# RWKV-7 branch of a hybrid decoder layer: the keys' norm applied in the channels' layout instead of at the evictions

## The chip, the cores and the metric

The kernel runs on one core of a Trainium2 chip. Its engines work side by side, each through its own list of instructions in order: TensorE (PE) multiplies matrices, VectorE (DVE) and ScalarE (ACT) work on elements, GpSimd (POOL) helps, and SyncE (SP) issues nearly all transfers (DMAs). The metric is the time of one execution in device microseconds (us).

## The reference

One step of one layer: 512 prompt tokens and 8 samples of 8 tokens (576 tokens in all) with 1024 channels. After a norm and one wide input projection, three branches run (RWKV-7, a gated linear recurrence, cross-attention), each with a gate; they are merged, projected and added to the input. The change lies in the RWKV-7 branch, which has 16 heads of 64 channels:

```python
kk = heads(k * k_k)
kk = kk * lax.rsqrt(jnp.sum(kk * kk, axis=-1, keepdims=True) + L2_EPS)   # norm over the 64 channels of a head
k = k * (1.0 + (a - 1.0) * k_a)
def step(s, inp):                       # per token; s is 64 x 64 for each head
    r_t, k_t, v_t, w_t, kk_t, a_t = inp
    sa = jnp.einsum("bhvk,bhk->bhv", s, -kk_t)
    s = s * w_t[:, :, None, :] + sa[..., None] * (kk_t * a_t)[:, :, None, :] + v_t[..., None] * k_t[:, :, None, :]
    return s, jnp.einsum("bhvk,bhk->bhv", s, r_t)
```

So each token and head has one number, the inverse squared norm of its key, that has to reach the products of kk. The kernel keeps kk without its norm on one side and multiplies that number in on the other.

## The kernel before

**Tiles.** The recurrence is done in 9 chunks of 64 tokens: 8 of the prompt, and one (c = 8) that holds the 8 samples. Heads go in pairs (a pair's 128 channels are the 128 partitions, tokens lie along the free axis); two pairs make a group, and four groups follow one another. For each group the program runs these stages, named as in the code:

- `prep_a`, for each pair: the low-rank products (`lora`, L909 and L910), tanh of them on ACT (L911), the running sum of the log decay as a scan on DVE (L914), its exponentials `pe` and `tw` on ACT (L918 to L920), the negated keys `lc` (L921) and their squares `sq` (L923).
- `prep_b`: nine matmuls per pair (`rs`, L932) sum the squares over the channels of a head. A token of the chunk is then a partition and (chunk, head) the free index, 64x18 in all. DVE turns the sums into `rsv`, the reciprocal with its factor (L935, L936). Then DVE builds `ZR` (L940 to L943) and `BK` (L944 to L948): the two sides of the chunk products.
- `prep_c`: `BKn`, the keys decayed to the chunk's end (L969 on ACT, the sample chunk at L970 on DVE), transposed on PE (`bkt`) beside the values (`vt`), in steps of 4, 4 and 1 chunks. ACT evicts `vt` (L977); DVE evicts `bkt` times `rsv` (L981), where the token is the partition again. Then the chunk products `m` (L990, four matmuls of 64x64x128 per chunk, 36 per pair) go to PSUM and DVE evicts them into `M1`, one 128x128 block at a time, times `rsv` of that token and head, times a mask (L996, 18 per pair).
- `invert`: the diagonal 32x32 blocks of `M1` go to DRAM and come back with one block per partition (L1006, L1011), are inverted by 60 small DVE operations (L1016, L1018) and written back (L1025 to L1032). Meanwhile `direct` (`R`, L1065, and `Zt`) and `bonus` run, and `invert2` finishes with `z` and `w` (L1041, L1050). Then the chain over the chunks follows, and at its end `gn_a`, the next group's `prep_a`, and `gn_t` and `gn_b`, which transpose, scale and gate the output (`ot`, `oT`): ACT evicts `oT` (L1240), POOL adds the bonus (L1245), DVE gates it (L1247), SP writes it out as `oad`.

**Filler.** All wide projections (input columns `u`, `za`, `g`, `br` and so on) are units of 48 matmuls at L355 (float32 split into a high and a low part). They do not depend on the recurrence, so `st.go(n)` and `st.until` place them between its stages to keep PE at work. Their weights come as `wraw` and are split by ACT (`whi`, L280) and DVE (`wlo`, L281).

**Order.** Each engine runs its own list in order. The build layer's scheduler sets these lists from the dependencies and its estimates, so the order of an engine's instructions is not that of the code. All PSUM tiles of the recurrence (`rs`, `lora`, `ot`, `vt`, `bkt`, `m`, `R`, `z`) take turns on four banks of one ring: a tile of this ring can only be written when the one four places earlier has been evicted.

Of the kernel before, what the change touches and what calls it, by code (L numbers as in the profile page):

```python
# [9 lines left out]
F32 = mybir.dt.float32  # L10
# [3 lines left out]
ALU = mybir.AluOpType  # L14
# [4 lines left out]
P = 128  # L19
# [5 lines left out]
N = TP + NB * NS  # L25
HN = N // 2
C = 64
NCH = N // C
# [6 lines left out]
L2_EPS = 1e-12  # L35
# [766 lines left out]
def rwkv_phase(K):  # L802
    nc, tc, i, pv, st = K.nc, K.tc, K.i, K.pv, K.st
    G = 2
# [3 lines left out]
    with ExitStack() as es:  # L808
# [9 lines left out]
        pe = [pe2[:, q, :] for q in range(G)]  # L818
        rsv = [rc.tile([P, NCH, 2], F32, name=f"rsv{q}") for q in range(G)]
        onat = rc.tile([P, NCH, P], F32, name="onat")  # L820
# [10 lines left out]
        for q in range(G):  # L831
            nc.gpsimd.memset(pe[q][:, 0:520].rearrange("p (c t) -> p c t", t=65)[:, :, 0:1], 1.0)
            nc.gpsimd.memset(pe[q][:, 520:592].rearrange("p (c t) -> p c t", t=9)[:, :, 0:1], 1.0)
            nc.gpsimd.memset(rsv[q][64 * q:64 * q + 64], 1.0)
            nc.gpsimd.memset(sbd[q], 0.0)
# [5 lines left out]
        x = (K.xh, K.xl)  # L841
# [39 lines left out]
        def chk(t):  # L881
            return t.rearrange("p (c t) -> p c t", t=C)
# [16 lines left out]
        def prep_a(o):  # L899
# [24 lines left out]
            o.pinv, o.zn, o.ta, o.sq = tw, lc, ta, sq  # L924

        def prep_b(o):
            p, q = o.p, o.q
            br = o.br
            zs = 1 - q
            pr_ = K.psb("rs")  # L930
            for c in range(NCH):
                nc.tensor.matmul(pr_[br:br + 64, 2 * c:2 * c + 2], o.sq[:, C * c:C * c + C], K.bones2, start=True, stop=True,  # L932
                                 tile_position=(0, br))
            rvf = rsv[q][br:br + 64].rearrange("p c h -> p (c h)")
            nc.vector.tensor_scalar(rvf, pr_[br:br + 64, 0:18], -2.0, -2.0 * L2_EPS, op0=ALU.mult, op1=ALU.add)  # L935
            nc.vector.reciprocal(rvf, rvf)  # L936
            BK = o.BK = rg.tile([P, NCH, 2, C], F32, tag="BK", name="BK")
# [5 lines left out]
            nc.vector.tensor_mul(ZR[:, 8, q, :].rearrange("p (b s) -> p b s", s=NS), smp(o.r), o.Ps[:, :, 1:])  # L943
            nc.vector.scalar_tensor_tensor(sq, ta, 1.0, zn, op0=ALU.add, op1=ALU.mult)  # L944
            nc.vector.tensor_mul(BK[:, :, zs, :], chk(sq), chk(o.pinv))
            nc.scalar.activation(ta, ta, AF.Identity, scale=K.kah[:, p:p + 1], bias=K.kac[:, p:p + 1])
# [16 lines left out]
        def prep_c(o):  # L963
            q, BK, ZR = o.q, o.BK, o.ZR
            rv = rsv[q]
            UV = o.UV = UV2[0][:, q]
# [6 lines left out]
            for c0, n in ((0, 4), (4, 4), (8, 1)):  # L973
# [5 lines left out]
                for c in range(c0, c0 + n):  # L979
                    K.transpose(pt[:, P * (c - c0):P * (c - c0) + P], BKn[:, c], P)  # L980
                nc.vector.tensor_mul(BKn[:, c0:c0 + n, :].rearrange("p c (h k) -> p (c h) k", h=2),  # L981
                                     pt[:, 0:P * n].rearrange("p (g k) -> p g k", k=C),
                                     rv[:, c0:c0 + n, :].rearrange("p c h -> p (c h)").unsqueeze(2).to_broadcast([P, 2 * n, C]))
            M1 = o.M1 = rg.tile([P, H2, P], F32, tag="M1", name="M1")
            for c0, n in ((0, 4), (4, 4), (8, 1)):
# [8 lines left out]
                for h in range(2):  # L994
                    for c in range(c0, c0 + n):
                        nc.vector.scalar_tensor_tensor(M1[:, 2 * c + h, :], pms[h][:, P * (c - c0):P * (c - c0) + P],  # L996
                                                       rv[:, c, h:h + 1], maskq[q][c == 8],
                                                       op0=ALU.mult, op1=ALU.mult)

# [508 lines left out]
```

## Time and profile before

| what | value |
|---|---|
| time, median of 3 runs | 1182.16 us (1181.98 to 1182.41) |
| the profiled execution | 1184.47 us, with a span of 1182.7 us |
| PE busy | 1145.4 us, 97% of the span |
| DVE busy | 713.2 us, 60% |
| ACT busy | 517.3 us, 44% |
| POOL busy | 184.3 us, 16% |
| first to last `rs` product | 276.8 us to 748.6 us |

The profile shows one execution. Busy time is the time in which an engine had an instruction under way; "idle before" is the time for which an instruction's engine had nothing to do ahead of it, with what released it. The span is from the first to the last instruction, and the 1.8 us beside it are start and end. A row of the trace gives its start in us, its length in us, the engine, the line of the code, and the tile written and the tiles read; "x4" stands for four like it in a row.

### The profile page before, as it was taken

What the parts mean: (1) busy time and instruction counts of PE and PEld (TensorE: products, weight loads), DVE (VectorE), ACT (ScalarE), POOL (GpSimd) and SP (SyncE); (2) the same over time, 40 slices, a digit from 0 to 9 for tenths busy, and PEclk for the clock granted to TensorE, in tenths of its full rate; (3) what the DMA queues carried; (4) which work ended last, traced back from release to release, by engine and by line L of the source; (5) the groups of instructions that cost most, each with busy time, mean ns of one, the idle gap of its engine ahead of it and who ended that gap; (6) DMA issues with size and microseconds to landing.
All of it is one profiled execution on the core that took longest, in us unless ns stands there. A gap on an engine that the chain in (4) does not pass through costs nothing.

```text
span 1182.7 us, 25731 instructions
## 1 busy us (share of the span) xinstructions
PE 1145.4 (97%) x10567; PEld 1068.8 (90%) x10567; DVE 713.2 (60%) x1436; ACT 517.3 (44%) x1004; POOL 184.3 (16%) x311
## 2 busy tenths in 40 slices
PE   6999999999999999999999999999999999979997
PEld 4998877899998898988989989999889999979997
DVE  5345655238764687835788457874455386975633
ACT  5444544337324374243752336532444266442333
POOL 3010001010003210022100130101211012570031
PEclk9999999999999999999999999999999999998999
DMA  4447685522452233532233522345337665348412
GB/s 140 130 145 233 211 254 189 162 81 66 107 140 73 65 93 82 142 89 70 78 92 120 145 73 65 106 125 149 85 90 232 203 195 170 104 115 261 117 45 81
DMA packets 220623, 151.50 MB, mean 128 GB/s; under 512 B 52640, under 2 KB 196106, under 8 KB 220506
## 3 DMA queue, kind: packets, MB, share of 16 engines
q1 hardware_dynamic: 217242, 146.87, 42.1%
q10 hardware_dynamic: 3264, 2.99, 0.9%
q8 instruction: 83, 1.36, 0.5%
q14 instruction: 34, 0.28, 0.1%
HBM read 120.82 MB, written 29.01 MB: 127 GB/s over the span
## 4 chain that ended last, share of the span: by engine, by line
PE 79%; DVE 7%; ACT 5%; issue 3%; DMA 3%; POOL 2%; SPq 0%; DVEq 0%; ACTq 0%; POOLq 0%
PE u L355 13%; PE g L355 12%; PE br L355 9%; PE xb L355 4%; PE zc L355 4%; PE za L355 4%; PE fo L1349 4%; PE q L355 4%; PE zb L355 3%; PE kv L355 2%; PE m L990 1%; PE dS L1137 1%; DVE wlo L281 1%; DMA wraw<-in_w_mem_kv 1%; PE skt L64 1%
## 5 line engine op out<-in xcount | busy, mean ns | idle before, releaser
L280 ACT CAST whi<-wraw 128x1024 fp32r<-128x1024 f32 x129 | 135.4, 1050 | 292.6 <-PE g L355 90.7
L281 DVE TENSOR_TENSOR wlo<-wraw,whi 128x1024 fp32r<-128x1024 f32 x128 | 158.9, 1241 | 127.5 <-ACT whi L280 126.7
L355 PE MATMUL u<-xh,whi 128*128 128x288 f32 x400 | 92.2, 305 | 0.0
L355 PE MATMUL br<-oh,wlo 128*128 128x288 f32 x384 | 84.4, 302 | 4.4 <-DVE wlo L281 4.3
L355 PE MATMUL u<-xl,whi 128*128 128x288 f32 x400 | 88.6, 300 | 0.0
L355 PE MATMUL u<-xh,wlo 128*128 128x288 f32 x400 | 88.6, 299 | 0.0
L355 PE MATMUL br<-oh,whi 128*128 128x288 f32 x384 | 85.4, 305 | 3.0 <-ACT oh L592 2.9
L355 PE MATMUL g<-xh,whi 128*128 128x288 f32 x384 | 86.6, 304 | 0.0
L355 PE MATMUL g<-xh,wlo 128*128 128x288 f32 x384 | 84.7, 300 | 0.0
L355 PE MATMUL g<-xl,whi 128*128 128x288 f32 x384 | 84.4, 301 | 0.0
L355 PE MATMUL br<-ol,whi 128*128 128x288 f32 x384 | 84.2, 301 | 0.0
L355 PEld LDWEIGHTS u<-xh,whi 128*128 128x128 f32 x400 | 65.1, 188 | 5.5 <-issue 4.1
L355 PEld LDWEIGHTS br<-oh,wlo 128*128 128x128 f32 x384 | 63.5, 194 | 5.6 <-DVE wlo L281 5.6
L355 PEld LDWEIGHTS br<-oh,whi 128*128 128x128 f32 x384 | 63.7, 193 | 4.3 <-ACT oh L592 3.4
L355 PEld LDWEIGHTS u<-xl,whi 128*128 128x128 f32 x400 | 64.7, 188 | 2.0 <-issue 1.4
L355 PEld LDWEIGHTS u<-xh,wlo 128*128 128x128 f32 x400 | 64.7, 188 | 0.9 <-issue 0.2
L355 PEld LDWEIGHTS g<-xh,whi 128*128 128x128 f32 x384 | 62.3, 190 | 3.2 <-issue 3.1
L355 PEld LDWEIGHTS g<-xh,wlo 128*128 128x128 f32 x384 | 62.7, 190 | 1.2 <-issue 1.2
L355 PEld LDWEIGHTS br<-ol,whi 128*128 128x128 f32 x384 | 63.4, 193 | 0.1
L355 PEld LDWEIGHTS g<-xl,whi 128*128 128x128 f32 x384 | 62.4, 190 | 1.1 <-issue 1.1
L1016 DVE TENSOR_TENSOR Xt<-X 72x30 f32<-72x30 f32 (+14 forms) x120 | 39.3, 328 | 11.4 <-DMA X<-d 7.8
L1349 PE MATMUL fo<-wol,oh 128*128 128x256 f32 (+1 forms) x160 | 45.0, 282 | 0.0
(386 smaller groups left out, 2894.3 us busy)
## 6 DMA issues: line engine op xcount, KB each, us to landing
wraw<-in_w_in SPq DMA_DIRECT2D x89, 512.0 KB
wraw<-in_w_mem_kv SPq DMA_DIRECT2D x16, 512.0 KB
kn<-in_cache_mem_k SPq DMA_DIRECT2D x16, 512.0 KB
kn<-in_cache_mem_v SPq DMA_DIRECT2D x16, 512.0 KB
gd<-flt SPq DMA_DIRECT2D x24, 288.0 KB
gtt<-gd SPq DMA_DIRECT2D x24, 288.0 KB
wraw<-in_w_br_c SPq DMA_DIRECT2D x8, 512.0 KB
wraw<-in_w_br_a SPq DMA_DIRECT2D x8, 512.0 KB
```

What stands on the lines that cost most here:

```text
L64: self.nc.tensor.transpose(out, in_, self.ident[:rows, :rows])
L280: nc.scalar.copy(hi, raw)
L281: eng.tensor_sub(lo, raw, hi.bitcast(F32))
L355: nc.tensor.matmul(self.ps[:, o:o + m], a[:, k, :], b[:, k, t0:t0 + m], start=(k == 0 and q == 0), stop=(k == KC - 1 and q == 2))
L990: nc.tensor.matmul(pms[h][64 * w:64 * w + 64, P * (c - c0):P * (c - c0) + P], BK[64 * h:64 * h + 64, c, w, :], ZR[64 * h:64 * h + 64, c].r ...
L1016: nc.vector.tensor_mul(tv, X[:, 0:s, s:s + 1].to_broadcast([NQ, s, m]), X[:, s:s + 1, s + 1:].to_broadcast([NQ, s, m]))
L1137: nc.tensor.matmul(pS[hs, C * o.q:C * o.q + C], o.BKn[:, c, hs], o.UV[:, c, hs], start=True, stop=True, tile_position=(0, 64 * h))
L1349: nc.tensor.matmul(pos[t][:r, :W], a[:, k, t * P:t * P + r], b[:, k, :], start=(k == 0 and q == 0), stop=(k == KC - 1 and q == 2))
```

## The change

It does three things.

1. The norm's reciprocal is applied once in the channels' layout. The nine `rs` matmuls, the scaling and the reciprocal move from `prep_b` to the end of `prep_a`. The result (64 tokens x 18) is written to a DRAM tile `d4` transposed (each of its 1152 elements goes to an address of its own; L936 in the changed file), and read back twice (L939), each time one head's row of 576 numbers spread over that head's 64 partitions, into the tile `sq`, whose squares are no longer needed. In `prep_b`, `sq` is multiplied by `pinv` (the tile `tw`), `(ta + 1) * zn` is written to `BK` directly, and `BK` is multiplied by `sq`: three DVE operations of 128x576 where there were two.
2. The eviction of the transposed `BKn` is a plain copy, and ACT does it (L989) instead of DVE.
3. The eviction of `m` into `M1` multiplies by the mask alone, four chunks at a time: 6 operations per pair (four of 128x4x128, two of 128x128; L1001) instead of 18.

`rsv` has its two heads outside the chunks now, and its initial fill with ones is gone.

```diff
--- before.py
+++ after.py
@@ -816,7 +816,7 @@
         ue = [rc.tile([P, UE], F32, name=f"ue{q}") for q in range(2)]
         pe2 = rc.tile([P, G, PE_], F32, name="pe")
         pe = [pe2[:, q, :] for q in range(G)]
-        rsv = [rc.tile([P, NCH, 2], F32, name=f"rsv{q}") for q in range(G)]
+        rsv = [rc.tile([P, 2, NCH], F32, name=f"rsv{q}") for q in range(G)]
         onat = rc.tile([P, NCH, P], F32, name="onat")
         sbd = [rc.tile([P, G, P], F32, name=f"sbd{r}") for r in range(2)]
         sbs = rc.tile([P, NB, P], F32, name="sbs")
@@ -831,7 +831,6 @@
         for q in range(G):
             nc.gpsimd.memset(pe[q][:, 0:520].rearrange("p (c t) -> p c t", t=65)[:, :, 0:1], 1.0)
             nc.gpsimd.memset(pe[q][:, 520:592].rearrange("p (c t) -> p c t", t=9)[:, :, 0:1], 1.0)
-            nc.gpsimd.memset(rsv[q][64 * q:64 * q + 64], 1.0)
             nc.gpsimd.memset(sbd[q], 0.0)
 
         xw2 = [rc.tile([P, N], F32R, name=f"xw{n}") for n in range(2)]
@@ -923,17 +922,26 @@
             nc.scalar.activation(sq, lc, AF.Square)
             o.pinv, o.zn, o.ta, o.sq = tw, lc, ta, sq
 
+            br = o.br
+            pr_ = K.psb("rs")
+            for c in range(NCH):
+                nc.tensor.matmul(pr_[br:br + 64, 2 * c:2 * c + 2], sq[:, C * c:C * c + C], K.bones2, start=True, stop=True,
+                   tile_position=(0, br))
+            rv = rsv[q][br:br + 64]
+            nc.vector.tensor_scalar(rv.rearrange("p h c -> p c h"), pr_[br:br + 64, 0:18].rearrange("p (c h) -> p c h", h=2),
+                                    -2.0, -2.0 * L2_EPS, op0=ALU.mult, op1=ALU.add)
+            rvf = rv.rearrange("p h c -> p (h c)")
+            nc.vector.reciprocal(rvf, rvf)
+            d4 = dr.tile([18, C], F32, tag="d4", name="d4")
+            nc.sync.dma_start(d4.rearrange("x t -> t x"), rvf)
+            d4h = d4.rearrange("(h c) t -> h (c t)", h=2)
+            for h in range(2):
+                nc.sync.dma_start(sq[64 * h:64 * h + 64, :], d4h[h:h + 1, :].to_broadcast([64, N]))
+
         def prep_b(o):
             p, q = o.p, o.q
             br = o.br
             zs = 1 - q
-            pr_ = K.psb("rs")
-            for c in range(NCH):
-                nc.tensor.matmul(pr_[br:br + 64, 2 * c:2 * c + 2], o.sq[:, C * c:C * c + C], K.bones2, start=True, stop=True,
-                                 tile_position=(0, br))
-            rvf = rsv[q][br:br + 64].rearrange("p c h -> p (c h)")
-            nc.vector.tensor_scalar(rvf, pr_[br:br + 64, 0:18], -2.0, -2.0 * L2_EPS, op0=ALU.mult, op1=ALU.add)
-            nc.vector.reciprocal(rvf, rvf)
             BK = o.BK = rg.tile([P, NCH, 2, C], F32, tag="BK", name="BK")
             ZR = o.ZR = rg.tile([P, NCH, 2, C], F32, tag="ZR", name="ZR")
             zn, ta, sq = o.zn, o.ta, o.sq
@@ -941,8 +949,9 @@
             nc.vector.tensor_mul(ZR[:, 8, zs, :].rearrange("p (b s) -> p b s", s=NS), smp(zn), o.Ps[:, :, 0:NS])
             nc.vector.tensor_mul(ZR[:, 0:8, q, :], chk(o.r)[:, 0:8, :], o.Pp[:, :, 1:])
             nc.vector.tensor_mul(ZR[:, 8, q, :].rearrange("p (b s) -> p b s", s=NS), smp(o.r), o.Ps[:, :, 1:])
-            nc.vector.scalar_tensor_tensor(sq, ta, 1.0, zn, op0=ALU.add, op1=ALU.mult)
-            nc.vector.tensor_mul(BK[:, :, zs, :], chk(sq), chk(o.pinv))
+            nc.vector.tensor_mul(sq, sq, o.pinv)
+            nc.vector.scalar_tensor_tensor(BK[:, :, zs, :], chk(ta), 1.0, chk(zn), op0=ALU.add, op1=ALU.mult)
+            nc.vector.tensor_mul(BK[:, :, zs, :], BK[:, :, zs, :], chk(sq))
             nc.scalar.activation(ta, ta, AF.Identity, scale=K.kah[:, p:p + 1], bias=K.kac[:, p:p + 1])
             nc.vector.tensor_mul(o.k, o.k, ta)
             nc.vector.tensor_mul(BK[:, :, q, :], chk(o.k), chk(o.pinv))
@@ -962,7 +971,6 @@
 
         def prep_c(o):
             q, BK, ZR = o.q, o.BK, o.ZR
-            rv = rsv[q]
             UV = o.UV = UV2[0][:, q]
             BKn = o.BKn = rg.tile([P, NCH, P], F32, tag="BKn", name="BKn")
             for c in range(8):
@@ -978,9 +986,7 @@
                 pt = K.psb("bkt")
                 for c in range(c0, c0 + n):
                     K.transpose(pt[:, P * (c - c0):P * (c - c0) + P], BKn[:, c], P)
-                nc.vector.tensor_mul(BKn[:, c0:c0 + n, :].rearrange("p c (h k) -> p (c h) k", h=2),
-                                     pt[:, 0:P * n].rearrange("p (g k) -> p g k", k=C),
-                                     rv[:, c0:c0 + n, :].rearrange("p c h -> p (c h)").unsqueeze(2).to_broadcast([P, 2 * n, C]))
+                nc.scalar.copy(BKn[:, c0:c0 + n, :].rearrange("p a b -> p (a b)"), pt[:, 0:P * n])
             M1 = o.M1 = rg.tile([P, H2, P], F32, tag="M1", name="M1")
             for c0, n in ((0, 4), (4, 4), (8, 1)):
                 pms = [K.psb("m1") for h in range(2)]
@@ -992,10 +998,9 @@
                                              ZR[64 * h:64 * h + 64, c].rearrange("p a b -> p (a b)"), start=True, stop=True,
                                              tile_position=(64 * h, 64 * w))
                 for h in range(2):
-                    for c in range(c0, c0 + n):
-                        nc.vector.scalar_tensor_tensor(M1[:, 2 * c + h, :], pms[h][:, P * (c - c0):P * (c - c0) + P],
-                                                       rv[:, c, h:h + 1], maskq[q][c == 8],
-                                                       op0=ALU.mult, op1=ALU.mult)
+                    nc.vector.tensor_mul(M1.rearrange("p (c h) m -> p c h m", h=2)[:, c0:c0 + n, h, :],
+                                         pms[h][:, 0:P * n].rearrange("p (c m) -> p c m", m=P),
+                                         maskq[q][c0 == 8].unsqueeze(1).to_broadcast([P, n, P]))
 
         def invert(prs):
```

What this does to the lists of the engines, shown for the second group (`rsv_2472` and `rsv_2473` belong to its first and second pair).

**The squares and the low-rank products on PE.** Before, around the first pair's `rs`:

```order
L355 MATMUL za_5041<-xl,whi 128x288 x2
L355 MATMUL za_5041<-xh,wlo 128x288 x2
L932 MATMUL rs<-bones_129,sq 64x2 x9
L355 MATMUL g_5126<-xh,whi 128x288 x2
L355 MATMUL g_5126<-xl,whi 128x288 x2
```

With the change:

```order
L355 MATMUL za_4932<-xh,wlo 128x288
L928 MATMUL rs<-bones_129,sq 64x2 x9
L908 MATMUL lora<-xw_2493,wls 128x288
L909 MATMUL lora<-xw_2493,wls 128x288
L908 MATMUL lora<-xw_2494,wls 128x288
L909 MATMUL lora<-xw_2494,wls 128x288
```

The first `rs` came after all 96 `za` matmuls; now it stands among the first 48, ahead of the second pair's `lora`. The second one stood 18 filler matmuls behind the first; now it stands eight `lora` and 41 filler matmuls behind it, ahead of `ot`, and 44 filler matmuls lie between `ot` and `vt`.

**SP around the new transfers.** Before:

```order
L60 DMA out_rwkv_p<-sf 64x64 x4
L60 DMA oad<-oT 128x576
L60 DMA wraw<-in_w_in 128x8x128
L60 DMA oad<-oT 128x576
L60 DMA wraw<-in_w_in 128x8x128
L60 DMA gd<-flt 128x576
L1006 DMA d_5489<-M_5235 32x18x32 x2
```

With the change:

```order
L60 DMA out_rwkv_p<-sf 64x64 x4
L936 DMA d_4928<-rsv_2472 64x18x1
L60 DMA wraw<-in_w_in 128x8x128
L939 DMA sq<-d_4928 64x576 x2
L936 DMA d_4990<-rsv_2473 64x18x1
L939 DMA sq<-d_4990 64x576 x2
L60 DMA oad<-oT 128x576
L60 DMA wraw<-in_w_in 128x8x128
L60 DMA oad<-oT 128x576
L60 DMA gd<-flt 128x576
```

Three transfers per pair stand ahead of both `oad` writes. The weight load that stood between these writes stands between the first pair's transfers now, and the next load between the writes. SP waits at each `L936` for the reciprocal and at each `L939` for the data of `L936`.

**DVE from the second reciprocal to the sample chunk's keys.** Before:

```order
L935 TENSOR_SCALAR rsv_2473<-rs 64x18
L944 SCALAR_TENSOR_TENSOR sq<-ta,lc 128x576
L936 RECIPROCAL rsv_2473<-rsv_2473 64x18
L945 TENSOR_TENSOR BK<-sq,tw 128x9x64
L970 TENSOR_TENSOR BKn<-BK,pe 128x128
L981 TENSOR_TENSOR BKn<-bkt,rsv_2472 128x512
L947 TENSOR_TENSOR k<-k,ta 128x576
L981 TENSOR_TENSOR BKn<-bkt,rsv_2472 128x512
L948 TENSOR_TENSOR BK<-k,tw 128x9x64
L949 TENSOR_TENSOR ta<-r,k 128x576
L981 TENSOR_TENSOR BKn<-bkt,rsv_2472 128x128
```

With the change:

```order
L934 RECIPROCAL rsv_2473<-rsv_2473 64x18
L952 TENSOR_TENSOR sq<-sq,tw 128x576
L949 TENSOR_TENSOR ZR<-lc,pe 128x64
L954 TENSOR_TENSOR BK<-BK,sq 128x9x64
L951 TENSOR_TENSOR ZR<-r,pe 128x64
L953 SCALAR_TENSOR_TENSOR BK<-ta,lc 128x9x64
L1252 SCALAR_TENSOR_TENSOR oT<-oT,tza 128x576
L1262 SCALAR_TENSOR_TENSOR tza<-tza,za_5057 128x576
L281 TENSOR_TENSOR wlo<-wraw,whi 128x1024
L1252 SCALAR_TENSOR_TENSOR oT<-oT,tza 128x576
L956 TENSOR_TENSOR k<-k,ta 128x576
L952 TENSOR_TENSOR sq<-sq,tw 128x576
```

Between these rows and the sample chunk's `BKn` of both pairs (L978, now one behind the other) there are three more operations of 128x576 (L957, L954, L958). For the first pair three operations stood between the second pair's scaling (L935) and its sample chunk's `BKn` (L970); now 16 stand between L931 and L978.

**The products on PE and who evicts them.** Before, the end of the first pair's products:

```order
L990 MATMUL m_5262<-ZR,BK 64x128
L990 MATMUL m_5263<-ZR,BK 64x128
L355 MATMUL g_5311<-xl,whi 128x288 x2
L990 MATMUL m_5288<-ZR,BK 64x128 x2
L355 MATMUL g_5311<-xh,wlo 128x288 x2
L355 MATMUL g_5311<-xh,whi 128x288 x2
L355 MATMUL g_5311<-xl,whi 128x288 x2
L355 MATMUL g_5311<-xh,wlo 128x288 x2
L990 MATMUL m_5289<-ZR,BK 64x128 x2
```

With the change:

```order
L996 MATMUL m_5270<-ZR,BK 64x128
L996 MATMUL m_5271<-ZR,BK 64x128
L996 MATMUL m_5270<-ZR,BK 64x128
L996 MATMUL m_5271<-ZR,BK 64x128
L355 MATMUL g_5131<-xh,wlo 128x288 x2
L355 MATMUL g_5293<-xh,whi 128x288 x2
```

Before, two or eight filler matmuls at a time stood between these product tiles. With the change the first pair's `m` stand in one run, with filler behind it. In the whole list there were 15 changes from filler to `m`, and there is 1 now; from `m` to filler there were 22, and there are 8.

## The prediction

> **What bounds the kernel now.** I read the page first, then what PE waited for, then windows and the chain of waits at the places that the change touches. The page's shares of busy time:
>
> ```profile
> span 1182.7 us, 25731 instructions
> ...
> PE 1145.4 (97%) x10567; PEld 1068.8 (90%) x10567; DVE 713.2 (60%) x1436; ACT 517.3 (44%) x1004; POOL 184.3 (16%) x311
> ```
>
> PE is idle for 1182.7 - 1145.4 = 37.3 us of the span. Work taken from DVE is thus worth nothing by itself; it counts where PE waits for it. The waits of PE (engine, what was late, us in total, times, the longest):
>
> ```profile
> PE m L990 <- DVE M L996: 2.3, 4, 0.6
> PE sO L752 <- DMA kn<-in_cache_mem_v: 2.0, 1, 2.0
> PE ot L64 <- ACT ta L911: 1.0, 3, 0.3
> PE m L990 <- DVE BKn L981: 0.5, 1, 0.5
> ```
>
> The change can touch three of these: 2.3 + 1.0 + 0.5 = **3.8 us**. All other idle time of PE lies in stages that it leaves alone. The windows show how full PE is between the second group's low-rank products and its R (415 to 461), and what short waits do to the granted clock (the column ahead of the last two):
>
> ```profile
> core 0: us, PE busy (x) PEld busy (x) DVE busy (x) ACT busy (x) POOL busy (x), PEclk, DMA share, GB/s
> 210.00:220.00 10.00, 7.99 (x61) 6.24 (x58) 1.22 (x1) 2.99 (x6) 0.23 (x2) 0.83 0.71 232
> 450.00:460.00 10.00, 9.36 (x123) 8.30 (x122) 8.79 (x25) 1.97 (x4) 0.00 (x0) 1.00 0.30 69
> 415.00:461.00 46.00, 45.04 (x449) 42.00 (x447) 38.94 (x84) 29.67 (x64) 3.90 (x5) 1.00 0.26 76
> ```
>
> ```profile
> 213.63 0.64 PE L752 MATMUL sO<-kn,pts 128*32 128x256 f32 x8 [2.01 <-DMA kn<-in_cache_mem_v]
> ...
> 456.14 0.44 PE L990 MATMUL m<-ZR,BK 64*64 64x128 f32 x4 [0.64 <-DVE M L996]
> ```
>
> In that stage PE is busy for 45.04 of 46 us, DVE for 38.94. The last rows are of the timeline: the wait of 2.0 us for `sO` ends at 213.6 in the first window, which ran at a mean clock of 0.83: 1 - 0.83 is 0.17, at half clock 0.34 of 10 us, so 3.4 us at half speed, a loss of 1.7. The wait of 0.6 us in the second window left the clock at 1.00. So a wait here costs its own length, up to somewhere between 0.6 and 2 us. From 2 us it may cost 1.7 more.
>
> (The Trainium skill, page "TensorE: Matmul & The Clock Gate", Part 1: The HAM clock gate, has the clock halve only after an idle window of about 3.4 us. By it a wait of 2.0 us would be free of that loss; the first window here shows it was not.)
>
> **The change, part by part.** *Filler visits on PE.* The second group's products in the chain (start, length, work):
>
> ```profile
> 443.44 2.82 PE m L990 x63
> 446.26 0.46 PE g L355 x2
> 446.72 0.37 PE m L990 x4
> 447.08 1.26 PE g L355 x8
> ...
> 454.96 1.05 DVE M L996 x4
> ...
> 466.62 36.80 PE g L355 x276
> ```
>
> A filler matmul takes 36.80/276 = 0.133 us, a product within a run 2.82/63 = 0.045. Four products and eight filler matmuls would take 4 x 0.045 + 8 x 0.133 = 1.24; as a visit they took 0.37 + 1.26 = 1.63. So a switch from filler to `m` and back costs 0.39. The order has 14 fewer of them: 14 x 0.39 = **5.4 us** saved. No matmul is added or removed.
>
> *DVE and ACT.* By groups of one form (operation, tiles, shapes, count, busy us, mean ns):
>
> ```profile
> L996 DVE SCALAR_TENSOR_TENSOR M<-m,rsv,mask 128x128 f32<-128x128 f32 x72 | 18.9, 342 | 0.0
> L996 DVE SCALAR_TENSOR_TENSOR M<-m,rsv,maskc 128x128 f32<-128x128 f32 x64 | 16.9, 343 | 0.3 <-PE m L990 0.3
> L981 DVE TENSOR_TENSOR BKn<-bkt,rsv 128x512 f32<-128x512 f32 x16 | 10.9, 686 | 2.0 <-PE bkt L64 1.2 <-PE vt L64 0.7
> L949 DVE TENSOR_TENSOR ta<-r,k 128x576 f32<-128x576 f32 x8 | 6.0, 751 | 0.0
> L977 ACT COPY UV<-vt 64x512 f32<-64x512 f32 x16 | 9.2, 576 | 14.2 <-PE vt L64 14.2
> ```
>
> Per pair DVE loses 18 evictions of 0.342, of which the neighbours overlap by about 0.08 (the chain's four took 1.05): 4.7 us. It gains four of 128x512, for which the nearest row is the other eviction of that size with two tiles as input, 0.686, and two small ones: 4 x 0.69 + 2 x 0.28 = 3.3, less overlap about 3.1 (at worst the four old ones again, 1.05 each). It also loses two `bkt` evictions (1.4) with a small one, and gains one multiplication of 0.75. That is near -2.3 per pair, -18 us in all. ACT gains the three `bkt` copies, 2 x 0.58 and a small one, 1.4 per pair, 11 us in all. With DVE at 38.94 of 46 us none of this sets the end directly. What it does is free the product banks sooner: the **3.8 us** of waits should go.
>
> *The squares, now early.* PE has to reach `rs` later than ACT has the squares. For the second group:
>
> ```profile
> 418.08 0.29 PE L910 MATMUL lora<-xw,wls 128*128 128x288 f32 x1
> 419.17 1.36 DVE L914 TENSOR_TENSOR_SCAN lc<-smask,tw 128x576 f32<-128x576 f32 x1
> 420.56 0.64 ACT L918 ACTIVATE pe<-lc 128x512 f32<-128x512 f32 x1 [0.42 <-DVE lc L914]
> 421.24 0.67 ACT L920 ACTIVATE tw<-lc 128x576 f32<-128x576 f32 x1
> 422.34 0.78 ACT L921 ACTIVATE lc<-k,nkk 128x576 f32<-128x576 f32 x1
> 423.54 0.68 ACT L923 ACTIVATE sq<-lc 128x576 f32<-128x576 f32 x1
> 432.07 1.21 PE L932 MATMUL rs<-bones,sq 128*64 128x2 f32 x18
> ```
>
> The scan ends at 420.53. Without the second pair's work between (it now comes later), the exponentials, keys and squares take 0.55 + 0.14 + 0.6 + 0.68 + 0.68, about 2.7, so the first squares are there at 423.2. PE has 34 filler matmuls between the first pair's last `lora` and `rs`: 418.08 + 35 x 0.133 = 422.7. PE waits some **0.6** with the signal. Before, `rs` came 8 us after the squares. The second `rs` stands 49 matmuls of 0.133 later (6.5 us), behind nine of 1.21/18 = 0.07; its squares have the tanh, a split of weights, the scan and the same 2.7 us in the way. Both come near 431, the squares 0 to 0.8 late: I take **0.4**. What lies after that on PE shifts with it.
>
> *The sample chunk's keys.* DVE gets to them 16 operations behind the second `rs`, and the first of the gating products there waits for POOL:
>
> ```profile
> 428.37 2.81 POOL L1245 TENSOR_TENSOR oT<-oT,bon 128x576 f32<-128x576 f32 x2 [9.89 <-ACT oT L1240]
> 430.00 1.79 DVE L1247 SCALAR_TENSOR_TENSOR oT<-oT,tza 128x576 f32<-128x576 f32 x1
> 436.75 0.75 DVE L1247 SCALAR_TENSOR_TENSOR oT<-oT,tza 128x576 f32<-128x576 f32 x1
> ```
>
> The second `rs` ends at about 432.3. The 16 operations and the `BKn` itself are 10 of 0.75, one of 1.21 and six of 0.2 to 0.7, about 10.4 with overlaps; the wait for POOL's addition, which starts behind the `oT` evictions of ACT, adds 1.0: 443.9 with the signal. PE has nine `ot` (1.0), 44 filler matmuls (5.9), 17 transposes (1.9) and 10 filler matmuls (1.3) until the sample chunk's `bkt`: 432.3 + 10.1 = 442.4, with a wait for a bank on the way 442.9. So it waits **1.1**; between 0.3 (no wait for POOL) and 2.1 (below). Behind it on PE stand all the products and the filler; nothing can overtake. The banks of `m` come into play because the run is unbroken: 16 products take 0.72, and the third pair of tiles needs the first one evicted, two operations of 0.69 and a signal behind 0.72, at 2.2, where PE would be at 1.44. That is 0 to 0.75 per pair of heads; waits ahead of the run use part of it up. I take 0.3 a group here.
>
> Groups 2 to 4 then wait 0.6 + 0.4 + 1.1 + 0.3 = 2.4 each. The first group has no `oT`, so its keys are early, but its filler is short: I take 0.6 + 0.55 at `rs` and 0.85 at the banks, 2.0. In all 3 x 2.4 + 2.0 = **9.2 us**.
>
> *The way by DRAM.* Six transfers per group are added on SP's queue. The trace has no transfer of single elements. What it has is a read and a write of 288 KB by way of DRAM:
>
> ```profile
> 311.29 0.31 SPq L1011 DMA_DIRECT2D X<-d  x1
> 314.40 0.19 DVE L1016 TENSOR_TENSOR Xt<-X 72x30 f32<-72x30 f32 x1 [1.71 <-DMA X<-d]
> ...
> 340.98 0.32 SPq L1026 DMA_DIRECT2D d<-X  x1
> 344.38 0.32 SPq L1032 DMA_DIRECT2D M<-d  x1
> ```
>
> From issue to use 3.1 us, and 3.4 from the write's issue to that of the dependent read: 6.5 us together, 5.3 if the write of only 4.6 KB is the shorter for it. Between the reciprocal (about 433.3) and the multiplication that needs it, DVE has eight operations of some 0.75, two small ones and the 1.0 for POOL: about **7 us**, 5.5 in the first group. So the trip is covered by DVE's own work and costs nothing, with little to spare; without that cover it would cost 6.5 a group, 26 us. While SP waits for it, the output of the last group and a load of weights stand behind:
>
> ```profile
> 437.52 0.34 SPq L60 DMA_DIRECT2D oad<-oT  x1
> 440.03 0.37 SPq L60 DMA_DIRECT2D wraw<-in_w_in  x1
> ```
>
> SP issues these at 437.5 anyway, when `oT` is there; the second pair's transfers are out by 433.5 + 3.4 = 437. No one waits for them sooner.
>
> (The Trainium skill, page "DMA: Bandwidth & Descriptors", section Rules for kernel authors, says that a transfer whose last dimension is not contiguous becomes one descriptor per element. That speaks against the write, with 1152 of them; no row here shows their price. The page's section Anatomy of one DMA gives some 2.0 us for one DMA plus its bytes; two in a row would take 4.0 by it and stay covered.)
>
> **The sum.** Removed 3.8 + 5.4 = 9.2; added 9.2. Against the profiled execution (1184.47 = 1182.7 + 1.8 around it) that is 0; the median shown is 2.3 below that execution, and I count from the median: 1182.2 + 0.1 for rounding, **1182.3 us**.
>
> **The rivals.**
>
> *A, faster: only the squares are waited for.* The POOL wait and DVE's overlaps are what the 1.1 rests on; DVE is relieved by 2.3 us per pair, so it may reach the sample chunk's keys in time, and the banks come free at 0.69 per four chunks. Then 1.0 in groups 2 to 4 and 1.1 in the first remain, 4.1 with the terms rounded, and the gain is 9.2 - 4.1 = 5.1: 1177.1 us. Against it: the 16 operations in the list.
>
> *B, slower: the sample chunk's keys late by over 2 us.* The row of 430.00 shows a gating product of 1.79 instead of 0.75 beside POOL's addition. The change puts both of these products in the path, ahead of the keys. If one is slowed so, the wait grows by 1.0 to 2.1, which passes the 2.0 that cost clock at 211: 3 x (1.0 + 1.7) = 8.1, 1190.4 us; 3.0 and 1185.3 without the clock. Against it: one slow row of eight positions cannot be told from a product that began early; the point from which it decides is a wait of 2 us.
>
> *C, slower: the way by DRAM is late.* It decides above 7 us (5.5 in the first group), and the rows give 5.3 to 6.5 without single elements. At 10 us it costs 3 x 3 + 4.5 = 13.5: 1195.8 us, with DVE idle at the multiplication by `tw` and PE behind it.
>
> **How the numbers follow.** No change 0.38, A 0.30, B 0.20, C 0.12. A measurement of this kernel can tell about 0.2%, 2.4 us, from no change; so the likeliest case reaches from 1179.9 to 1184.6. The range takes in A and B with their neighbours and leaves out most of C: 1177.0 to 1190.0. Faster by over 0.2%: 0.30, within it 0.38, slower 0.32.
>
> **What would show it.** In the changed profile: PE's waits for `sq` of 0.4 to 0.6 at `rs`, for the sample chunk's `BKn` of about 1 at `bkt` in three groups, and none for L996. An eviction L1001 near 0.69. One run of `m` per pair. The multiplication of `sq` by `tw` not waiting for a DMA (C if it does). No half clock at 440 to 450 (B if there is). The second group's R, which began here, at about the same time:
>
> ```profile
> 461.13 2.31 PE L1065 MATMUL R<-UV,M 64*64 64x64 f32 x72
> ```
>
> If it moves by less than 1 us, the sum of the first two groups is right; the later ones should move it no further. I am wrong if an end of the chain that I took as covered moves: the return of the inverted blocks or the weights' splits.

## The result, and the profile after

The changed kernel takes 1237.95 us (median of 4 runs, 1235.24 to 1244.54) against 1182.29 us before: 1.0474 times as long (95% interval 1.043 to 1.0519), 55.7 us slower. The page of the profiled execution (1236.78 us):

```profile
span 1235.1 us, 25657 instructions
...
PE 1156.5 (94%) x10567; PEld 1078.8 (87%) x10567; DVE 690.2 (56%) x1324; ACT 529.2 (43%) x1028; POOL 182.0 (15%) x309
```

DVE and ACT moved about as forecast: 713.2 - 690.2 = 23.0 less on DVE (18 forecast), 529.2 - 517.3 = 11.9 more on ACT (11). PE is idle for 78.6 us where it was 37.3. PE's busy time also grew by 11.1, with the same number of matmuls: more of them ran at half clock (the mean granted clock of this execution is 0.975; it was 0.992). The waits (what was waited for, us in total, times, longest):

```profile
PE bkt L64 <- ACT BKn L977: 25.9, 6, 8.3
...
PE m L996 <- DVE M L1001: 6.5, 6, 5.6
...
PE rs L928 <- ACT sq L922: 5.5, 8, 0.8
PE bkt L64 <- DVE BKn L978: 4.4, 1, 4.4
...
DVE sq L952 <- DMA sq<-d: 46.7, 8, 11.1
```

The last row is the source: DVE waits in all eight pairs, 46.7 us in all, for the spread reciprocals to come back from DRAM. ACT's `BKn` and PE's `bkt` wait behind it. The chain of waits in the second group gives the length of each leg:

```profile
441.66 11.94 DMA d<-rsv
...
454.18 4.01 DMA sq<-d
...
463.33 4.23 DMA sq<-d
```

The write takes 11.94 us from its issue to its landing, the read 4.01. SP's queue and DVE show how the two pairs follow each other (start, length, engine, line, work, and the idle time before it):

```profile
441.66 0.61 SPq L936 DMA_DIRECT2D d<-rsv  x1
443.83 0.37 SPq L60 DMA_DIRECT2D wraw<-in_w_in  x1
453.66 1.11 SPq L939 DMA_DIRECT2D sq<-d  x2
454.86 0.62 SPq L936 DMA_DIRECT2D d<-rsv  x1
462.82 1.09 SPq L939 DMA_DIRECT2D sq<-d  x2
```

```profile
450.47 0.25 DVE L934 RECIPROCAL rsv<-rsv 64x18 f32<-64x18 f32 x1
458.28 0.76 DVE L952 TENSOR_TENSOR sq<-sq,tw 128x576 f32<-128x576 f32 x1 [7.57 <-DMA sq<-d]
467.65 0.76 DVE L952 TENSOR_TENSOR sq<-sq,tw 128x576 f32<-128x576 f32 x1 [3.20 <-DMA sq<-d]
```

The second pair's reciprocal is there at 450.7, but SP stands at the first pair's reads until 453.66 and issues the second write at 454.86. From that reciprocal to the product that needs it pass 16.9 us.

The evictions themselves cost what was forecast, 0.684 for a four-chunk eviction of `M` and 0.584 for a copy of `BKn`:

```profile
L1001 DVE TENSOR_TENSOR M<-m,mask 128x512 f32<-128x512 f32 x16 | 10.2, 684 | 6.0 <-PE m L996 6.0
...
L989 ACT COPY BKn<-bkt 128x512 f32<-128x512 f32 x16 | 9.3, 584 | 2.1 <-PE bkt L64 2.0
```

### The profile page after: what moved, and what is told of

Its sections match the earlier page's. It is cut to its first block, busy times and chain, and to the rows that moved or that the text cites. A ratio compares the mean times of both kernels' runs of the same rounds, so it can differ in the third digit from the quotient of the medians.

```text
span 1235.1 us, 25657 instructions
## 1 busy us (share of the span) xinstructions
PE 1156.5 (94%) x10567; PEld 1078.8 (87%) x10567; DVE 690.2 (56%) x1324; ACT 529.2 (43%) x1028; POOL 182.0 (15%) x309
## 4 chain that ended last, share of the span: by engine, by line
PE 67%; DMA 10%; DVE 9%; ACT 7%; issue 5%; POOL 1%; SPq 0%; DVEq 0%; ACTq 0%
PE u L355 11%; PE g L355 10%; PE br L355 7%; DMA d<-rsv 4%; PE fo L1354 4%; PE zc L355 4%; PE xb L355 3%; PE q L355 3%; PE zb L355 3%; DMA sq<-d 3%; PE kv L355 3%; DVE wlo L281 2%; PE m L996 2%; PE dS L1142 1%; ACT whi L280 1%
## 5 line engine op out<-in xcount | busy, mean ns | idle before, releaser
L64 PE MATMUL bkt<-ident,BKn 128*128 128x128 f32 x72 | 18.5, 356 | 30.3 <-ACT BKn L977 25.9
```

What stands on the lines that cost most here:

```text
L64: self.nc.tensor.transpose(out, in_, self.ident[:rows, :rows])
```

## The experiments

Three questions: is the way by DRAM the whole loss; what in it costs; and where did the forecast gain of 9.2 us go?

**1. Without the way by DRAM.**

```diff
-            d4 = dr.tile([18, C], F32, tag="d4", name="d4")
-            nc.sync.dma_start(d4.rearrange("x t -> t x"), rvf)
-            d4h = d4.rearrange("(h c) t -> h (c t)", h=2)
-            for h in range(2):
-                nc.sync.dma_start(sq[64 * h:64 * h + 64, :], d4h[h:h + 1, :].to_broadcast([64, N]))
-            nc.scalar.activation(sq, lc, AF.Square)
+            nc.scalar.activation(sq, lc, AF.Square, scale=0.01)
```

> The changed kernel without the way by DRAM: the reciprocals are computed, but neither written out nor read back, so the tile sq keeps the squares (scaled by 0.0001, so that all stays finite) and the norm is left out of the result. Theory 1, the loss is the way by DRAM: what is left is the forecast's other terms, 9.2 us of waits added and 9.2 taken away, so 1177 to 1185 us, with PE's waits for the sample chunk's BKn near 1 us. Rival, the loss comes from the early squares, or from ACT taking over the BKn evictions: it stays above 1200 us.

Measured: 1195.06 us, 1.0106 times the time before (1.0086 to 1.0125). So 1237.95 - 1195.06 = 42.9 us are the way by DRAM, and 12.8 us are something else: neither theory. PE's waits, and the second group from R to R, before and here:

```profile
PE m L991 <- DVE M L996: 5.4, 11, 1.3
PE rs L928 <- ACT sq L922: 4.8, 8, 0.8
```

```profile
461.13:616.23 155.10, 153.69 (x1657) 143.07 (x1656) 102.44 (x234) 69.02 (x143) 22.55 (x35) 1.00 0.34 93
```

```profile
463.39:620.97 157.58, 153.31 (x1656) 142.63 (x1656) 97.23 (x206) 71.69 (x148) 23.68 (x35) 1.00 0.33 92
```

The group is 2.5 us longer, though PE has 0.4 less to do in it. DVE has 5.2 less to do, which is worth nothing here. The waits for the squares are 0.6 each, as forecast. Products wait for their banks 11 times, 5.4 us, where it was 2.3 in 4 waits. The scheduler also orders this run anew: its PE list has 4 changes from filler to `m` where the changed kernel has 1, and the wait for the sample chunk's keys, forecast near 1 us in three groups, is one of 0.2. So the 42.9 compare two orders; the next run has the changed kernel's.

**2. The write in rows.** The same transfers, in the same order on all engines, but the write has 64 rows of 72 bytes in place of 1152 single elements.

```diff
-            d4 = dr.tile([18, C], F32, tag="d4", name="d4")
-            nc.sync.dma_start(d4.rearrange("x t -> t x"), rvf)
-            d4h = d4.rearrange("(h c) t -> h (c t)", h=2)
+            d4 = dr.tile([C, 18], F32, tag="d4", name="d4")
+            nc.sync.dma_start(d4, rvf)
+            d4h = d4.rearrange("(h t) x -> h (t x)", h=2)
```

> The changed kernel with the 64x18 reciprocals written as 64 rows of 72 bytes instead of 1152 single elements; read back as before, so that scales reach the wrong tokens. All engines' orders are the same. Theory 1a, each single element costs: from the write's issue to the issue of the reads some 3.4 us instead of 8.3 to 12.5, the first pair's multiplication waits no longer, and the time falls to 1182 to 1195 us. Rival 1b, any write to DRAM takes that long here, or the queue's weight load of 512 KB between is what delays it: 1230 to 1240 us as before.

Measured: 1197.54 us (one run), 40.4 us less than the changed kernel. SP in the second group:

```profile
425.76 0.45 SPq L936 DMA_DIRECT2D d<-rsv  x1
...
428.40 1.19 SPq L939 DMA_DIRECT2D sq<-d  x2
434.86 0.46 SPq L936 DMA_DIRECT2D d<-rsv  x1
436.60 1.08 SPq L939 DMA_DIRECT2D sq<-d  x2
```

From the write's issue to that of the reads it takes 2.6 and 1.7 us where it was 12.0 and 8.0, and DVE no longer waits for `sq` at all. The weight load is still issued between the first pair's write and its reads, at 427.94. It is neither the way by DRAM as such nor that load: it is the single elements. With the way covered, this run also shows the changed order by itself, as the forecast had assumed it:

```profile
438.37 1.97 DVE L1252 SCALAR_TENSOR_TENSOR oT<-oT,tza 128x576 f32<-128x576 f32 x1 [1.32 <-POOL oT L1250]
```

```profile
446.50 0.45 PE L64 MATMUL bkt<-ident,BKn 128*128 128x128 f32 x1 [2.47 <-ACT BKn L977]
```

```profile
440.00:450.00 10.00, 7.53 (x100) 7.11 (x99) 7.64 (x13) 7.63 (x22) 0.00 (x0) 0.83 0.35 114
```

DVE waits 1.32 us for POOL's addition, and the gating product takes 1.97 in place of 0.75. The sample chunk's transposition comes 2.47 us late (the row names ACT's `BKn`; what ended last for c = 8 is DVE's L978, at 446.5), and a window of 3.4 us at half clock follows: 0.83 over these ten. The same wait comes in three groups, 7.4 us in all.

**3. The write twice**, once for each head's read.

```diff
-            nc.sync.dma_start(d4.rearrange("x t -> t x"), rvf)
+            for h in range(2):                      # d4s: two DRAM tiles; head h's read takes d4s[h]
+                nc.sync.dma_start(d4s[h].rearrange("x t -> t x"), rvf)
```

> The changed kernel with the transposed element write done twice, to two DRAM tiles, one for each head's read. Theory 1a, the price is per element: 8.3 to 12.5 us from the first write's issue to the reads become 15 to 22, and the eight trips add 50 to 90 us: 1285 to 1325 us. Rival 1b, a fixed price per way: only the second issue of 0.6 us is added, 1237 to 1250 us.

Measured: 1306.16 us (one run), 68.2 us more than with one write.

```profile
456.72 1.38 SPq L937 DMA_DIRECT2D d<-rsv  x2
...
468.32 9.82 SPq L940 DMA_DIRECT2D sq<-d  x2
478.26 2.30 SPq L937 DMA_DIRECT2D d<-rsv  x2
489.63 5.88 SPq L940 DMA_DIRECT2D sq<-d  x2
```

```profile
DVE sq L953 <- DMA sq<-d: 102.9, 8, 18.4
```

The first read is issued 11.6 us after the first write, about as with one. The second read needs the second write. It is out at 468.32 + 9.82 = 478.14; less its own issue of 0.48, it is issued 20.9 us after the first write in this pair, 16.8 in the next one. Over the eight pairs this is 15.2 to 21.1 us, where the changed kernel took 8.0 to 12.5 with one write: 8.1 us more in the mean (5.2 to 10.4). So a second write of 1152 elements costs some 8 us of its own, 7 ns per element: theory 1a, in its time and in its 15 to 22 us.

The number of pieces alone does not set this price. In the kernel before, the blocks of `M1` are written by two transfers of 32x18 pieces of 128 bytes, also 1152 pieces, with a weight load behind them:

```profile
306.49 1.05 SPq L1006 DMA_DIRECT2D d<-M  x2
...
311.29 0.31 SPq L1011 DMA_DIRECT2D X<-d  x1
```

The read that needs them is issued 4.8 us after the first of them, and 4.1 to 4.5 us in the other groups. Whether 4 bytes are slow because they are so few, or because neighbouring words in DRAM come from different partitions here, no run separates.

**4. The write left in, and read by no one.**

```diff
-            d4h = d4.rearrange("(h c) t -> h (c t)", h=2)
+            d4h = d5.rearrange("(h c) t -> h (c t)", h=2)     # d5: constants, written at the start
```

> The changed kernel with the element write left in place but its tile read by no one: the two spreading reads take constants that were written to DRAM at the start, so the result lacks the norm. Reads wait only for the rs matmuls to be done with the squares. Theory 1: the read's 3 to 4.6 us is covered by DVE's work and the time is 1177 to 1190 us. Rival, the read leg or the transfers' load on the queue is what costs: above 1200 us.

Measured: 1225.04 us (one run). The time is the rival's. Nobody needs the elements, and 1225.04 - 1195.06 = 30 us of the 42.9 are still lost; the reads themselves are not the reason, since experiment 2 has them too. In the second group SP issues one read, the element write, then the other read:

```profile
437.28 0.61 SPq L940 DMA_DIRECT2D d<-rsv  x1
437.93 0.72 SPq L943 DMA_DIRECT2D sq<-d  x1
```

```profile
448.99 0.76 DVE L956 TENSOR_TENSOR sq<-sq,tw 128x576 f32<-128x576 f32 x1 [7.03 <-DMA sq<-d]
```

The read issued behind the elements is there for DVE at 448.99, 11.1 us after its issue, where a read took 4.01 in the changed kernel. What stands behind the elements is held up.

**5. The same with the element write on another queue.**

```diff
-            nc.sync.dma_start(d4.rearrange("x t -> t x"), rvf)
+            nc.scalar.dma_start(d4.rearrange("x t -> t x"), rvf)
```

> The run in which the reads take constants and the element write is read by no one (1225 us), with that write issued from ACT's queue instead of SP's; the norm is left out of the result. Theory 3a, the elements hold up what stands behind them in their own queue: the reads and weight loads on SP's queue pass them, the multiplication by tw waits less than 1 us, 1193 to 1203 us. Rival 3b, they hold up the DMA engines for every queue: 1215 to 1230 us as on SP.

Measured: 1221.17 us (one run): rival 3b. One run each cannot tell this from the 1225.04 on SP's queue. The windows after the write of the second group (issued from ACT at 436.40; the last three columns are the clock, the share of the DMA engines' time and GB/s):

```profile
437.00:439.00 2.00, 2.00 (x17) 2.00 (x16) 1.65 (x3) 1.93 (x5) 0.00 (x0) 1.00 0.69 150
439.00:440.00 1.00, 1.00 (x10) 1.00 (x9) 1.00 (x1) 0.65 (x1) 0.00 (x0) 1.00 0.09 4
440.00:449.00 9.00, 8.68 (x77) 8.43 (x76) 7.02 (x15) 7.41 (x16) 1.59 (x2) 1.00 0.27 34
449.00:451.00 2.00, 2.00 (x17) 2.00 (x16) 0.00 (x0) 2.00 (x7) 1.23 (x1) 1.00 0.95 241
```

SP had issued a weight load of 512 KB at 438.57. Over nine us it moves at 34 GB/s. Then, at 449, the transfers run at 241. The load's packets take 11.2 us in all; behind the pieces of 128 bytes in the kernel before, the same load took 3.2. In the trace's packet records the 4-byte packets run from 438.3 to 439.3 (1168 of them), so what lasts ten us comes after they were recorded. The DMA engines are recorded busy for 0.27 of that time only, and what they wait for is not shown. What is shown is that transfers of the other queue are slowed as well.

**6. The early squares alone**, in the kernel before: only the place of `rs`, scaling and reciprocal is changed.

```diff
             o.pinv, o.zn, o.ta, o.sq = tw, lc, ta, sq
+            br = o.br
+            pr_ = K.psb("rs")
+            for c in range(NCH):
...
+            nc.vector.reciprocal(rvf, rvf)
 
         def prep_b(o):
...
-            nc.vector.reciprocal(rvf, rvf)
```

> The kernel before with one edit: the rs matmuls, the scaling and the reciprocal stand at the end of prep_a, as in the change; the norm is applied at the evictions as before, so the result is complete. Theory 2a, of the 12.8 us that are left without the way by DRAM, about 4.8 are PE's waits for the early squares (4.8 us in 8 waits in that run): 1186 to 1190 us, with waits of rs for sq near 0.6 each. Rival 2b, the early squares cost nothing since filler that stood ahead of them is only moved, and the 12.8 us come from the evictions: 1181 to 1184 us.

Measured: 1196.0 us, 1.0103 (1.0081 to 1.0124). That is as much as experiment 1 had left over, and more than theory 2a gave it (1186 to 1190):

```profile
PE m L991 <- DVE BKn L982: 5.7, 3, 1.9
PE rs L928 <- ACT sq L923: 5.5, 8, 0.8
...
PE m L991 <- DVE M L997: 4.9, 7, 1.0
```

The waits for the squares are the one half. The other is that DVE comes late to evict the transposed `BKn` (L982 here) and the products wait for its bank, 1.9 us in three groups. With the change this eviction is ACT's, so this half is not the same wait as in experiment 1. The next run therefore takes the early squares out of that one.

**7. Late squares, with the rest of the change**, and no way by DRAM.

```diff
         def prep_a(o):
...
-            nc.vector.reciprocal(rvf, rvf)
 
         def prep_b(o):
...
+            pr_ = K.psb("rs")
+            for c in range(NCH):
...
+            nc.vector.reciprocal(rvf, rvf)
```

> The run without the way by DRAM, with the rs matmuls, the scaling and the reciprocal back in prep_b; BKn copied by ACT and M evicted four chunks at a time with the mask alone stay, and the norm is left out of the result. Theory 2a: the 4.8 us of waits for the squares go and 1188 to 1191 us remain, from products that come in one run and wait for their banks (5.4 us in 11 waits before). Rival 2b: 1193 to 1196 us, as with the early squares.

Measured: 1188.62 us, 1.0033 (1.0018 to 1.0048): theory 2a, and some 8.6 us below experiment 1, by the ratios (0.0073 of 1182; by the two intervals, 6 to 11). The squares' place thus carries about two thirds of the 12.8. PE's waits for them are 4.8 of the 8.6. In the profiled executions PE was also busy for 1146.3 - 1141.6 = 4.7 us longer in experiment 1, with as many matmuls and at a mean granted clock of 0.987 against 0.992; no run ties that to the squares.

What is left stands in the third group. In the profiled execution its R starts 0.3 us earlier than in the kernel before. From there to the next R, before and here:

```profile
616.23:772.80 156.57, 154.73 (x1657) 143.66 (x1656) 108.02 (x242) 69.11 (x143) 23.08 (x34) 1.00 0.37 103
```

```profile
615.96:776.47 160.51, 154.91 (x1656) 144.26 (x1655) 104.76 (x216) 71.48 (x148) 24.50 (x34) 0.99 0.36 100
```

That is 3.9 us longer, the 0.0033. In it lies a wait of 2.8 us for `z` (below), which the kernel before had not, and a stretch of 3.4 us at half clock behind it. `z` waits for the return of the inverted blocks, one of the two ends of the chain that the prediction named as its signs of being wrong.

**8. Late squares and 18 evictions of M.**

```diff
-                    nc.vector.tensor_mul(M1.rearrange("p (c h) m -> p c h m", h=2)[:, c0:c0 + n, h, :],
-                                         pms[h][:, 0:P * n].rearrange("p (c m) -> p c m", m=P),
-                                         maskq[q][c0 == 8].unsqueeze(1).to_broadcast([P, n, P]))
+                    for c in range(c0, c0 + n):
+                        nc.vector.tensor_mul(M1[:, 2 * c + h, :], pms[h][:, P * (c - c0):P * (c - c0) + P], maskq[q][c == 8])
```

> As the run before it, with the squares late, and in addition M evicted one 128x128 block at a time again (18 per pair, with the mask alone, the norm left out of the result), so that the order puts filler between the products again (9 changes from filler to m, where the four-chunk form had 1). Of the change only the BKn copy on ACT and the multiplications in the channels' layout are left. Theory 2a, the products' run costs what filler visits save: 1181 to 1186 us, waits of m below 3 us. Rival 2c, ACT's copies are what costs: 1188 to 1192 us as with four chunks at a time.

Measured: 1185.77 us, 1.002 (1.0007 to 1.0033). The intervals of this run and the last overlap, so four chunks at a time against one is not told apart. The time lies in theory 2a's range. The products' waits in the two:

```profile
PE m L990 <- DVE M L995: 4.1, 11, 1.2
...
PE z L1040 <- DMA xz<-d: 2.8, 1, 2.8
```

```profile
PE m L990 <- DVE M L996: 4.6, 8, 1.1
```

With 18 evictions and filler between the products PE waits as long as without: theory 2a's "below 3 us", its reason, does not hold. Neither form takes away the waits that the kernel before had, and neither run is below its time.

**9. and 10. The sums spread by PE.** The complete change without DRAM, with late squares: each channel gets the sum of its head from a product with the block matrix of ones, and the reciprocal is taken over 128x576. In the second of them M is evicted in 18 pieces.

```diff
+                nc.tensor.matmul(pr_, K.bones, o.sq[:, cs], start=True, stop=True)
+                nc.vector.tensor_scalar(rv[:, cs], pr_, -2.0, -2.0 * L2_EPS, op0=ALU.mult, op1=ALU.add)
+            nc.vector.reciprocal(rv, rv)
```

> The whole change with the way by DRAM replaced: two matmuls of 128x288 per pair against the block matrix of ones give each channel the sum over its head (the squares rounded to the matmul's float32r form by ACT), at the place of the late squares; DVE scales two halves and takes the reciprocal over 128x576. Nothing is left out but the rounding. Theory: no wait for a DMA; PE spends 2 x 0.133 per pair instead of 18 small matmuls' 0.6, 2.7 us less in all, against the 3.9 us that the late squares with four chunks at a time measured: 1182 to 1187 us. Rival: the wider reciprocal on DVE (128x576, not seen so far) delays the sample chunk's keys: above 1190 us.

> As the run before it, with M evicted one 128x128 block at a time (mask alone). Theory: 2.4 us as measured with late squares and 18 evictions, less 2.7 us of PE: 1180 to 1185 us, no difference from before that can be told. Rival, as above: over 1188 us.

Measured: 1193.33 us, 1.0079 (1.0062 to 1.0096), and 1198.31 us, 1.0128 (1.0105 to 1.015). Of the first:

```profile
L935 DVE RECIPROCAL sqs<-sqs 128x576 f32<-128x576 f32 x8 | 29.9, 3741 | 0.0
```

Both times are the rival's: a reciprocal over 128x576 takes 3.74 us, five times a product of that size (0.74), and 30 us of DVE's time stand in front of `BK` and `BKn`. PE waits for `BKn` at `bkt` for 3.6 + 2.2 us, where experiment 7 has no such wait. The second form's products wait longer (6.4 us against 3.9); the rest of the 5 us between the two is not explained. The first is the quickest complete form of the change here, 44.6 us below the one with the way by DRAM, and still slower than the kernel before.

## Why the prediction was wrong

**The way by DRAM** is the step that failed, and with it the sum: 42.9 of the 55.7 us. I took 5.3 to 6.5 us for the trip, from transfers of the same 288 KB in long rows, and held it covered by 7 us of DVE's work. The write leg alone measured 11.94 us, and 2.6 or 1.7 when the same numbers went out as rows. The rows were far from it in what costs: pieces of 4 bytes. The nearest row in the trace was another, the 1152 pieces of 128 bytes of L1006, which I did not look at; with its 4.1 to 4.8 us and the 3.1 of the read the trip is 7.2 to 7.9, no longer covered by 7. I had no row for single elements and so should have kept the upper end open; I let the write's 4.6 KB speak for the lower end instead. Rival C was this mechanism, with the right place and the right trace in the profile, but I priced it at 10 us a trip and at a chance of 0.12. Measured from reciprocal to product, the trip took 16.7 us for the first pair of the second group and 16.9 for the second. Rival C priced one trip in a group where both pairs make one, the second pair's write waiting on SP for the first pair's reads, and it left out the clock: behind waits of several us PE ran at half clock (0.975 in the mean).

The rule that I quoted from the Trainium skill, "DMA: Bandwidth & Descriptors", section Rules for kernel authors (one descriptor per element where the last dimension is not contiguous), speaks of just this write, and the trace agrees: experiment 5 records 1168 packets of 4 bytes behind the issue of the 1152 elements. The page's fixed 2.0 us per DMA, which I set beside it, is given there for transfers that GpSimd issues; the write in rows, issued by SP, came near it (its reads went out after 1.7 and 2.6 us), and the write of single elements did not.

**That a stall elsewhere is covered if DVE has work** was the second error in this step. Experiment 4 shows that even unread elements cost 30 us, because they hold up reads and weight loads behind them. I had asked who waits on SP's queue, and not what the transfers do to each other.

**The sample chunk's keys**: 1.1 us forecast, 2.47 measured in experiment 2, where the trip was covered as I had assumed. This is rival B as I had described it, a gating product slowed beside POOL (1.97) and a wait past 2 us with half clock behind it. Its whole price was forecast at 1190.4 us; experiment 2 took 1197.54. So without the elements the forecast would have been wrong too, on the same side.

**The squares**: 0.6 + 0.4 us forecast in a group, 4.1 in all; 0.6 for each of eight in experiment 1, 4.8. The waits were right, a little small. But by experiments 1 and 7 the squares' place costs some 8.6, twice the term. One part that the forecast held at nothing is the clock: it read from one row that a wait of 0.6 us is free of half clock, and some waits of 0.7 us were not (last section).

**The gain of 9.2 us** did not come. Of the visits' 5.4 us I had 4 x 0.39 = 1.6 in a group with four. From the second R to the third PE's busy time fell from 153.69 by 0.4 in experiment 1, which has one visit left there, and by 0.55, to 153.14, in experiment 7, which has none. What a visit costs was read from its rows in the chain, and most of that does not vanish with it. The 3.8 us of waits did not go but moved: products that come in one run wait for the banks of their own evictions, 5.4 us in experiment 1 and 4.1 in experiment 7. I had priced these banks at 0.3 per group.

**What was right**: the durations of the new evictions, DVE's relief and ACT's load, that DVE's relief is worth nothing by itself, and the signs to look for.

What stays open: the last 2.4 us of experiment 8 (late squares, 18 evictions, copies on ACT, one multiplication more on DVE), whose lower end, 0.0007, is close to nothing; why the inverted blocks make PE wait in the third group of experiment 7; and where the elements spend their ten us after their packets were recorded.

## What to carry to other kernels

Price a transfer by its pieces before its bytes: look at the number and the size of the contiguous runs on its smaller side, and if no row of the trace has pieces that small, leave the cost open upwards. Here 1152 pieces of 4 bytes took 8 to 12.5 us where 1152 of 128 bytes took under 5. The write of single elements also slowed transfers on the other queue, so hiding its latency was not enough. And before moving a step earlier in an in-order list, write down what the engine now meets before its old next step: the squares' new place cost some 8.6 us, about the whole gain that had been forecast.

## What the runs showed that was not expected

Single elements of 4 bytes: some 7 ns each (experiment 3), and some ten us in which a weight load moves at 34 GB/s in place of 241 (experiment 5).

Half clock after a wait is a matter of chance at this length. In experiment 6 the same wait came in three groups, 1.90, 1.88 and 1.89 us long; the windows after them:

```profile
447.00:457.00 10.00, 7.14 (x102) 6.00 (x101) 10.00 (x27) 5.25 (x13) 0.00 (x0) 1.00 0.12 44
606.00:616.00 10.00, 8.12 (x100) 7.04 (x100) 9.73 (x27) 4.71 (x11) 0.00 (x0) 0.83 0.09 34
765.00:775.00 10.00, 7.14 (x102) 6.00 (x101) 9.81 (x29) 5.40 (x14) 0.00 (x0) 1.00 0.23 78
```

Only the second lost clock. Shorter waits lost it too: in the changed kernel PE waited 0.72 us for the second pair's squares until 448.53, and then:

```profile
450.00:453.00 3.00, 3.00 (x16) 3.00 (x15) 0.71 (x2) 2.52 (x6) 0.21 (x1) 0.51 0.31 26
```

Across the profiled executions of all kernels here, from 200 us on, a stretch at half clock began no later than 3.4 us behind 7 of the 48 waits of over 0.5 us for early squares (all 7 were of 0.7 to 0.9 us), and behind 32 of the 35 waits of 2 to 3 us. But for the last one of an execution, each stretch is 3.41 us long or a multiple of that. The Trainium skill, "TensorE: Matmul & The Clock Gate", Part 1: The HAM clock gate, describes a window that runs on by itself, which fits that equal waits differ; its idle window of about 3.4 us does not, since 1.88 us were enough once.

A reciprocal on DVE takes 0.25 us for 18 numbers per partition and 3.74 for 576: 6.5 ns per number, where a product of that size takes 0.75 / 576 = 1.3.
